# Second MLP product run one Strassen product after the other, with PSUM sums over the whole contraction and eight units begun early

## Chip, cores and metric

The kernel runs on one core of a Trainium2 chip. The metric is the device time of one launch in microseconds (us); lower is better.

## What is computed

A trunk of two layers over 1040 tokens (16 meta tokens and 1024 of the sequence): an SSD mixer and an MLP, then latent attention (MLA) and a second MLP. All is float32. The change touches the two MLPs only.

```python
D_MODEL = 1024; D_FF = 4 * D_MODEL
def sqrelu_mlp(h, w_up, w_down):
    return jnp.square(jax.nn.relu(h @ w_up)) @ w_down
# per layer:  h = h + mixer(rms_norm(h, ln_mix));  h = h + sqrelu_mlp(rms_norm(h, ln_mlp), w_up, w_down)
# out = h[:, N_META:]
```

## The kernel before

**Strassen.** `mlp(layer, ...)` (L557) forms each of its two products with the Winograd form of Strassen's scheme: both operands are cut in 2 x 2 blocks, and seven products P1 to P7 of blocks and of sums of blocks are made in place of eight. The token axis is cut in two halves of n columns (520 in layer 0, as two pieces of 260; 512 in layer 1). Each float32 product is three fp32r matmuls (L602 to L604: hi x hi, hi x lo, lo x hi), so every operand is split into a rounded part hi (ScalarE casts: L594 for weights, L743 for activations) and a rest lo (a subtraction: L596 for weights, in turn on GpSimd and VectorE; L744 for activations, on GpSimd).

**Up part.** 16 units of 256 hidden rows; each runs its seven products over 4 chunks of 128, that is 24 matmuls of 260 columns a product in layer 0 and 12 of 512 columns in layer 1. The weight loads (`raw`, L637), all hidden stores (L673, L688 to L695, into `hid`) and every other DMA of the MLP are issued by SyncE's queue, in order. Before the units can run, the head of the MLP has to make the sums of the activation blocks for P4 to P7 (`x_sums`, L797 to L817, with four lo parts on GpSimd a call, L744) while TensorE runs P1 and P2 of the first NPRE = 4 units, whose operands are plain blocks; GpSimd also sums the squares for the norm there (L754). P1's result waits in SBUF (`pu`, NPRE + 1 buffers) till the unit is finished later.

**Down part.** The contraction over 4096 hidden rows is cut in five parts of 4, 4, 3, 3 and 2 unit rows (DCH). In each part all seven products run (DORDER), each into PSUM tiles of its own (`mps`; four in layer 0, eight in layer 1), and each result is moved into the SBUF sums M: a copy in the first part (L1007), an addition on VectorE in the others (L1009), the joining sums of the last part on VectorE and GpSimd (L1014, L1032). The residual is added by VectorE from a DMA copy in layer 0 (L979, L980), and in layer 1 by matmuls with an identity ahead of the first part's products P2 to P5 (L997), whose tiles `ht` are loaded by DMA and partly changed on VectorE (L993, L995). Sums of weight blocks s1 and s2 are made on VectorE (L928 to L934) and kept in SBUF. The hidden block of a product is loaded (L901), cast as one instruction of 4n columns a lane (L903), and its lo part taken as one instruction too (L904), on GpSimd for five products of seven.

The order of each engine's queue comes from a scheduler that sorts the program by what is ready; `ahead` (L965) prepares weights four items ahead, loads twelve.

## Time and profile before

| | us |
|---|---|
| median of 3 runs | 3090.19 (3084.61 to 3090.22) |
| profiled execution | 3085.05 |
| its span | 3083.3 |
| TensorE busy in the span | 2924.2 (95%) |
| VectorE / GpSimd / ScalarE busy | 2365.5 / 1479.9 / 1298.1 |

MLP of layer 0: head from 976, units to about 1325, down part to 1695. MLP of layer 1: head from 2385, units to about 2715, down part to 3083. In the rows a chunk of time is given from the start of the span; "PEclk" is the granted TensorE clock as a share of full speed (2.4 GHz); a busy TensorE isn't a TensorE at its full rate, so a stretch is read by its number of matmuls too.

### The profile page before, as it was taken

The page shows a single profiled execution, that of the slowest core. Times are in us where ns is not written, and L with a number is a line of the kernel's source. Part 1 is how long each engine was busy: PE and PEld are TensorE (multiplying, and loading weights), DVE is VectorE, ACT ScalarE, POOL GpSimd, SP SyncE. Part 2 cuts the span into 40 slices and gives each one's busy share as a digit, 9 for nine tenths or more (in the row PEclk, how much of TensorE's full clock was granted, in tenths as well). Part 3 has the DMA queues.
Part 4 walks back from the last instruction along what each step waited for, and adds up shares of the span by engine and source line. Part 5 has one row for each costly group of instructions (what it writes and reads, how often), then busy time and mean ns, then how long its engine had stood idle before and what let it go on. Part 6 is the DMA issues. An engine that isn't in the chain of part 4 may idle for free.

```text
span 3083.3 us, 48544 instructions
## 1 busy us (share of the span) xinstructions
PE 2924.2 (95%) x18221; PEld 2604.8 (84%) x18221; DVE 2365.5 (77%) x3843; ACT 1298.1 (42%) x2453; POOL 1479.9 (48%) x1168
## 2 busy tenths in 40 slices
PE   7999999999999899999998889999999899989998
PEld 7999999998899799999998777777777688867886
DVE  6677887778667877777879477877865899865778
ACT  4343433334424433344332546655543533344342
POOL 2344544446746422245556454553655622243556
PEclk9999999999999899999999989999999899999999
DMA  3333433335533344464532201101223354464342
GB/s 107 70 75 68 77 66 74 74 74 130 153 97 118 117 160 142 149 234 143 169 119 85 60 22 26 26 25 27 92 80 100 99 191 161 154 231 158 121 146 96
DMA packets 290997, 332.72 MB, mean 108 GB/s; under 512 B 29981, under 2 KB 189682, under 8 KB 290762
## 3 DMA queue, kind: packets, MB, share of 16 engines
q1 hardware_dynamic: 290762, 329.62, 36.1%
q8 instruction: 144, 2.36, 0.3%
q14 instruction: 91, 0.75, 0.1%
HBM read 240.43 MB, written 89.07 MB: 107 GB/s over the span
## 4 chain that ended last, share of the span: by engine, by line
PE 69%; DVE 19%; DMA 4%; issue 4%; ACT 2%; POOL 2%; SPq 0%; DVEq 0%; ACTq 0%; POOLq 0%
PE mps L602 8%; PE mps L604 8%; PE mps L603 8%; PE psm L98 6%; PE psm L100 6%; PE psm L99 6%; PE mps L1058 2%; PE mps L1059 2%; PE mps L1060 2%; DVE em L378 2%; DVE whl L596 1%; PE ppv L1440 1%; PE pst L1426 1%; DVE xT L244 1%; DVE mP L1009 1%
## 5 line engine op out<-in xcount | busy, mean ns | idle before, releaser
L602 PE MATMUL mps<-hhl,whl 128*128 128x260 f32 (+1 forms) x1472 | 447.7, 304 | 25.0 <-DVE mP L1009 19.0
L603 PE MATMUL mps<-hhl,whl 128*128 128x260 f32 (+1 forms) x1472 | 443.8, 302 | 1.5 <-POOL hhl L744 1.5
L604 PE MATMUL mps<-hhl,whl 128*128 128x260 f32 (+1 forms) x1472 | 441.6, 301 | 2.4 <-DVE whl L596 2.1
L98 PE MATMUL psm<-hn,whl 128*128 128x346 f32 (+4 forms) x1176 | 387.4, 330 | 1.9 <-ACT hn L220 1.2
L99 PE MATMUL psm<-hn,whl 128*128 128x346 f32 (+4 forms) x1176 | 384.9, 328 | 0.3 <-DVE hn L221 0.3
L100 PE MATMUL psm<-hn,whl 128*128 128x346 f32 (+4 forms) x1176 | 380.9, 325 | 1.1 <-POOL whl L93 1.1
L602 PEld LDWEIGHTS mps<-hhl,whl 128*128 128x128 f32 x1472 | 283.9, 193 | 37.5 <-issue 17.7
L604 PEld LDWEIGHTS mps<-hhl,whl 128*128 128x128 f32 x1472 | 284.7, 194 | 11.1 <-DVE whl L596 3.2
L603 PEld LDWEIGHTS mps<-hhl,whl 128*128 128x128 f32 x1472 | 283.9, 193 | 11.0 <-POOL hhl L744 3.0
L93 POOL TENSOR_TENSOR whl<-wraw,whl 128x1024 fp32r<-128x1024 f32 (+3 forms) x95 | 221.6, 2334 | 142.3 <-ACT whl L90 135.9
L602 PE MATMUL mps<-xP,whl 128*128 128x260 f32 (+1 forms) x768 | 252.7, 329 | 17.5 <-ACT xP L743 7.6
L603 PE MATMUL mps<-xP,whl 128*128 128x260 f32 (+1 forms) x768 | 251.9, 328 | 2.1 <-POOL xP L744 2.1
L604 PE MATMUL mps<-xP,whl 128*128 128x260 f32 (+1 forms) x768 | 250.5, 326 | 0.9 <-DVE whl L596 0.9
L596 POOL TENSOR_TENSOR whl<-s,whl 128x512 fp32r<-128x512 f32 (+2 forms) x84 | 119.5, 1422 | 252.3 <-ACT whl L594 162.9
L98 PEld LDWEIGHTS psm<-hn,whl 128*128 128x128 f32 (+1 forms) x1176 | 219.4, 187 | 9.8 <-ACT btk L397 3.5
L904 POOL TENSOR_TENSOR hhl<-raw,hhl 128x2080 fp32r<-128x2080 f32 (+5 forms) x50 | 199.3, 3986 | 55.7 <-ACT hhl L903 49.6
L100 PEld LDWEIGHTS psm<-hn,whl 128*128 128x128 f32 (+1 forms) x1176 | 219.3, 187 | 6.2 <-issue 3.3
L99 PEld LDWEIGHTS psm<-hn,whl 128*128 128x128 f32 (+1 forms) x1176 | 219.8, 187 | 4.8 <-issue 1.7
L596 POOL TENSOR_TENSOR whl<-draw,whl 128x512 fp32r<-128x512 f32 (+2 forms) x90 | 123.8, 1379 | 184.7 <-ACT whl L594 142.2
L596 POOL TENSOR_TENSOR whl<-raw,whl 128x512 fp32r<-128x512 f32 x64 | 96.3, 1507 | 239.0 <-ACT whl L594 128.9
L594 ACT CAST whl<-draw 128x512 fp32r<-128x512 f32 (+2 forms) x180 | 102.4, 574 | 214.0 <-PE mps L1060 107.4
L1058 PE MATMUL mps<-whl,hhl 128*128 128x512 f32 x448 | 177.9, 402 | 15.2 <-DVE mP L1009 9.6
(388 smaller groups left out, 8498.0 us busy)
## 6 DMA issues: line engine op xcount, KB each, us to landing
raw<-in_mlp_w_up_dram SPq DMA_DIRECT2D x32, 1024.0 KB
hid<-stg SPq DMA_DIRECT2D x96, 260.0 KB
wraw<-in_ssd_w_in_dram SPq DMA_DIRECT2D x48, 512.0 KB
hid<-stg SPq DMA_DIRECT2D x96, 256.0 KB
acsb<-acs_d SPq DMA_DIRECT2D x64, 256.0 KB
draw<-in_mlp_w_down_dram SPq DMA_DIRECT2D x16, 1024.0 KB
raw<-hid SPq DMA_DIRECT2D x14, 1040.0 KB
raw<-hid SPq DMA_DIRECT2D x14, 1024.0 KB
```

The lines of the kernel that those rows point to most:

```text
L93: eng_lo.tensor_tensor(lo, src, hi.bitcast(F32), ALU.subtract)
L98: PE.matmul(ps, whi, xhi, start=i == 0, stop=False)
L99: PE.matmul(ps, whi, xlo, start=False, stop=False)
L100: PE.matmul(ps, wlo, xhi, start=False, stop=i == n - 1)
L378: V.tensor_tensor(em[:n, :, :n], em[:n, :, :n], cbm[:n, :n].unsqueeze(1).to_broadcast([n, HPG, n]), ALU.mult)
L594: S.copy(wt[:, 0], src)
L596: (G if lo_n[0] % 2 else V).tensor_tensor(wt[:, 1], src, wt[:, 0].bitcast(F32), ALU.subtract)
L602: PE.matmul(ps[:, i, :], wt[:, 0, k, :], xt[:, k, 0, xs_], start=first, stop=False)
L603: PE.matmul(ps[:, i, :], wt[:, 0, k, :], xt[:, k, 1, xs_], start=False, stop=False)
L604: PE.matmul(ps[:, i, :], wt[:, 1, k, :], xt[:, k, 0, xs_], start=False, stop=last)
L904: (G if p not in ("P5", "P6") else V).tensor_tensor(xt[:, :, 1, :], raw, xt[:, :, 0, :].bitcast(F32), ALU.subtract)
L1058: PE.matmul(ps[:, 0, :], xt[:, k, 0, qs], wt[:, 0, 0, :], start=k == 0 and not res, stop=False)
```

## The change

Parts of the diff; the old down part (L865 to L1083) is shown above and goes entirely.

```diff
-    DCH = (4, 4, 3, 3, 2)
-    NPRE = 4
+    NC = 4
+    HOME = {"P2": (0, 0), "P3": (0, 1), "P4": (1, 0), "P5": (1, 1)}
+    NPRE = 8
...
+        p1_d = dram.tile([NPRE, P, n], F32, name=f"p1_{layer}")
...
-        def w_item(src):
+        def w_item(src, on_v=False):
...
-            (G if lo_n[0] % 2 else V).tensor_tensor(wt[:, 1], src, wt[:, 0].bitcast(F32), ALU.subtract)
+            (G if lo_n[0] % 2 and not on_v else V).tensor_tensor(wt[:, 1], src, wt[:, 0].bitcast(F32), ALU.subtract)
...
             def prep(self, p):
+                if p == "P6" and self.u < NPRE:
+                    self.p1 = pu()
+                    nc.sync.dma_start(self.p1, p1_d[self.u])
...
                     S.copy(v3(self.p1), ps)
+                    if self.u < NPRE:
+                        nc.sync.dma_start(p1_d[self.u], self.p1)
...
-            if i % 2:
-                x_sums(i // 2)
+            if i % 4 == 3:
+                x_sums(i // 4)
...
+        if by_tok:
+            PHASES = [([A11], {"P1": (0, [])}),
+                      ([A21, A22, A11], {"P6": (2, [(0, 0, 1, ADD, None), (2, 0, 2, SUB, "s2")]), "P5": (0, [])}),
+                      ([A11, A21, A22], {"P7": (0, [(0, 0, 1, SUB, None)]), "P4": (2, [])}),
+                      ([A12, "s2"], {"P2": (0, []), "P3": (1, [(1, 0, 1, SUB, None)])})]
+        else:
+            PHASES = [([A11], {"P1": (0, [])}), ([A11, A21], {"P7": (0, [(0, 0, 1, SUB, "s3")])}),
+                      ([A12], {"P2": (0, [])}), ([A22, "s3"], {"P6": (0, [(0, 0, 1, SUB, "s2")])}),
+                      ([A22], {"P4": (0, [])}), ([A21, A22], {"P5": (0, [(0, 0, 1, ADD, None)])}),
+                      ([A12, "s2"], {"P3": (0, [(0, 0, 1, SUB, None)])})]
...
+        drb = dn.enter_context(tc.tile_pool(reuse_waits="tile", name="drawb", bufs=2))
...
+        drp = [dn.enter_context(tc.tile_pool(reuse_waits="tile", name=f"draw{i}", bufs=1)) for i in range(5)]
...
+                if isinstance(what, str):
+                    nc.sync.dma_start(t, s_d[what][c])
+                else:
+                    rows = w_down[layer, c * 1024:(c + 1) * 1024, what[0] * 512:(what[0] + 1) * 512]
+                    nc.sync.dma_start(t, rows.rearrange("(k j p) m -> j p k m", p=P, j=2)[what[1]])
...
+            for k in range(4):
+                S.copy(xt[:, k, 0, :], raw[:, k, :])
+                V.tensor_tensor(xt[:, k, 1, :], raw[:, k, :], xt[:, k, 0, :].bitcast(F32), ALU.subtract)
...
+            for o, a_, b_, op, keep in sums:
+                V.tensor_tensor(r[o], r[a_], r[b_], op)
+                if keep and i == 3:
+                    nc.sync.dma_start(s_d[keep][c], R[f, c][o])
+            return w_item(r[mine], True)
...
+            while dpos[0] < min(groups.index((f, c)) + (2 if by_tok else 3), len(groups)):
+                dload(*groups[dpos[0]])
...
+            while dpos[1] < min(j + 2, len(prods)):
+                hload(*prods[dpos[1]])
...
+            if j == 1 and not by_tok:
+                for p_, (i, half) in HOME.items():
+                    nc.sync.dma_start(M[p_], hsp[:, 4 * i:4 * i + 4, half, :])
+            if by_tok and c == 1 and p in HOME:
+                for q in range(4):
+                    residual(p, q, ps[q])
```

Eight units instead of four have P1 and P2 run in the head. P1's result goes to DRAM (`p1_d`) and comes back when the unit is finished. The four calls of `x_sums` are spread over sixteen products instead of eight.

The down part now runs in phases (a phase holds one product, or two in layer 1); in each, the contraction is taken in NC = 4 chunks of four unit rows into the same four PSUM tiles, and the tile is moved out once, in the last chunk (`evict`). A weight block is loaded again in every phase that uses it: 44 loads of 1024 KB in layer 0 and 36 in layer 1, where before each of the four blocks was loaded once, in five pieces. s2 (both layers) and s3 = A11 - A21 (layer 0) are stored to DRAM, four stores each, and loaded again; these loads are among the 44 and 36. All lo parts of the down part are taken on VectorE, those of the hidden blocks as four instructions. In layer 0 the residual is loaded into M ahead of the sums; in layer 1 its matmuls stand in the second chunk.

In these rows `raw` is a block loaded by DMA, `whl` and `hhl` are split weights and activations, `xP` the split activations of P4, P5 and P7 (P6's are in `hhl`), `t`, `ta` and `tb` activation sums, `rb` the sum of squares.

GpSimd in the head of layer 0's MLP, from the second call of `x_sums` on. Before:

```order
L754 TENSOR_TENSOR rb<-rb,sq 128x520
L596 TENSOR_TENSOR whl<-s_10722,whl 128x512
L754 TENSOR_TENSOR rb<-rb,sq 128x520
L744 TENSOR_TENSOR xP_10318<-t_10541,xP_10318 128x520
L754 TENSOR_TENSOR rb<-rb,sq 128x520
L744 TENSOR_TENSOR hhl<-t_10542,hhl 128x520
L596 TENSOR_TENSOR whl<-s_10720,whl 128x512
L754 TENSOR_TENSOR rb<-rb,sq 128x520
L744 TENSOR_TENSOR xP_10319<-tb,xP_10319 128x520
L744 TENSOR_TENSOR xP_10317<-ta,xP_10317 128x520
L596 TENSOR_TENSOR whl<-s_10722,whl 128x512
L744 TENSOR_TENSOR xP_10318<-t_10618,xP_10318 128x520
```

Now:

```order
L767 TENSOR_TENSOR rb<-rb,sq 128x520
L598 TENSOR_TENSOR whl<-raw,whl 128x512
L767 TENSOR_TENSOR rb<-rb,sq 128x520
L757 TENSOR_TENSOR xP_10321<-t_10680,xP_10321 128x520
L767 TENSOR_TENSOR rb<-rb,sq 128x520
L757 TENSOR_TENSOR hhl<-t_10681,hhl 128x520
L598 TENSOR_TENSOR whl<-raw,whl 128x512
L767 TENSOR_TENSOR rb<-rb,sq 128x520
L757 TENSOR_TENSOR xP_10317<-ta,xP_10317 128x520
L757 TENSOR_TENSOR xP_10325<-tb,xP_10325 128x520
L598 TENSOR_TENSOR whl<-raw,whl 128x512
L757 TENSOR_TENSOR xP_10321<-t_10831,xP_10321 128x520
```

The sixteen L744 (now L757) and seven L754 (now L767) are the same; four lo parts of P1 weights of units 4 to 7 (L598 from `raw`) now stand between the sums, where the lo parts of unit 0's sums `s` stood, which come later.

VectorE inside the down part of layer 0; before in the second part (P4, P2's residual, P5, P3), where `mP` are the sums M and `mps` PSUM tiles:

```order
L596 TENSOR_TENSOR whl<-draw,whl 128x512
L1009 TENSOR_TENSOR mP_14376<-mP_14376,mps 128x520
L934 TENSOR_TENSOR draw<-draw,s_14383 128x4x128 x2
L1009 TENSOR_TENSOR mP_14376<-mP_14376,mps 128x520
L596 TENSOR_TENSOR whl<-draw,whl 128x512
L934 TENSOR_TENSOR draw<-draw,s_14383 128x4x128
L1009 TENSOR_TENSOR mP_14376<-mP_14376,mps 128x520
L1009 TENSOR_TENSOR mP_14372<-mP_14372,mps 128x520
L596 TENSOR_TENSOR whl<-s_14383,whl 128x512
L1009 TENSOR_TENSOR mP_14372<-mP_14372,mps 128x520
L980 TENSOR_TENSOR mP_14372<-mP_14372,raw 128x2080
L1009 TENSOR_TENSOR mP_14372<-mP_14372,mps 128x520
```

Now, in the phase of P2 and P6, L947 being the weight sums:

```order
L598 TENSOR_TENSOR whl<-draw,whl 128x512
L947 TENSOR_TENSOR draw<-draw,drawb 128x4x128 x4
L598 TENSOR_TENSOR whl<-draw,whl 128x512 x3
L939 TENSOR_TENSOR hhl<-raw,hhl 128x520 x4
L598 TENSOR_TENSOR whl<-draw,whl 128x512
L947 TENSOR_TENSOR draw<-draw,drawb 128x4x128 x4
L598 TENSOR_TENSOR whl<-draw,whl 128x512 x3
L939 TENSOR_TENSOR hhl<-raw,hhl 128x520 x3
L995 TENSOR_TENSOR mP_14418<-mP_14418,mps 128x520
L939 TENSOR_TENSOR hhl<-raw,hhl 128x520
L598 TENSOR_TENSOR whl<-draw,whl 128x512
L995 TENSOR_TENSOR mP_14418<-mP_14418,mps 128x520
```

An M addition (L1009) per PSUM tile stood between the lo parts; now lo parts of weights (L598) and of hidden blocks (L939) and the sums follow each other, and additions (L995) come with a product's last chunk only.

SyncE's queue where layer 0 goes from the units to the down part; before, with L895 the weight blocks, L901 the hidden blocks, and L673 to L695 the last units' stores:

```order
L895 DMA draw<-in_mlp_w_down_dram 128x4x512 x2
L673 DMA hid_4_10286<-stg 128x520
L895 DMA draw<-in_mlp_w_down_dram 128x4x512 x2
L901 DMA raw<-hid_0_10282 128x4x520
L895 DMA draw<-in_mlp_w_down_dram 128x4x512
L901 DMA raw<-hid_0_10282 128x4x520
L673 DMA hid_4_10286<-stg 128x520
L688 DMA hid_4_10286<-stg 128x520
L690 DMA hid_4_10286<-stg 128x520
L692 DMA hid_4_10286<-stg 128x520
L695 DMA hid_4_10286<-stg 128x520
L895 DMA draw<-in_mlp_w_down_dram 128x4x512
```

Now:

```order
L928 DMA drawb<-in_mlp_w_down_dram 128x4x512
L706 DMA hid_3_10285<-stg 128x520
L928 DMA draw<-in_mlp_w_down_dram 128x4x512
L933 DMA raw<-hid_1_10283 128x4x520
L928 DMA draw<-in_mlp_w_down_dram 128x4x512
L928 DMA drawb<-in_mlp_w_down_dram 128x4x512
L949 DMA s_0_14448<-draw 128x2048
L933 DMA raw<-hid_2_10284 128x4x520
L1052 DMA mP_14418<-hsp_10287 128x4x520
L1052 DMA mP_14419<-hsp_10287 128x4x520
L1052 DMA mP_14420<-hsp_10287 128x4x520
L1052 DMA mP_14421<-hsp_10287 128x4x520
```

Behind the last unit's stores stand the blocks of the P7 phase (L928, two a chunk), the s3 store (L949) and the four loads of M (L1052), with the next hidden blocks (L933) among them.

## Rows read from the trace of the kernel before

**Rows 1.** The page: busy time of TensorE, PEld its weight loads.

```profile
PE 2924.2 (95%) x18221; PEld 2604.8 (84%) x18221; DVE 2365.5 (77%) x3843; ACT 1298.1 (42%) x2453; POOL 1479.9 (48%) x1168
```

**Rows 2.** Windows: length, each engine's busy time (instructions), PEclk, DMA share, GB/s.

```profile
976.00:1077.00 101.00, 86.40 (x580) 81.32 (x579) 90.24 (x104) 54.85 (x89) 59.46 (x36) 0.85 0.37 125
1077.00:1308.00 231.00, 231.00 (x1928) 231.00 (x1927) 180.20 (x263) 81.66 (x138) 59.92 (x40) 1.00 0.45 152
1308.00:1389.00 81.00, 74.67 (x580) 73.72 (x579) 58.93 (x55) 37.24 (x53) 37.81 (x16) 0.94 0.65 227
...
1500.00:1585.00 85.00, 78.21 (x615) 77.67 (x615) 69.15 (x77) 29.44 (x42) 43.71 (x24) 0.94 0.54 175
1585.00:1695.00 110.00, 98.11 (x772) 96.78 (x770) 95.45 (x132) 34.33 (x60) 67.88 (x46) 0.95 0.30 87
2385.00:2456.00 71.00, 60.00 (x198) 40.44 (x197) 64.05 (x66) 43.40 (x71) 51.47 (x32) 0.78 0.34 111
2456.00:2696.00 240.00, 240.00 (x1061) 198.72 (x1060) 213.62 (x304) 89.16 (x156) 63.05 (x44) 1.00 0.49 164
2696.00:2762.00 66.00, 53.27 (x225) 43.78 (x224) 43.70 (x49) 24.80 (x35) 29.16 (x11) 0.90 0.70 251
2762.00:2848.00 86.00, 79.51 (x385) 66.36 (x384) 44.33 (x40) 36.92 (x52) 36.45 (x17) 0.96 0.50 159
...
3044.00:3083.00 39.00, 25.53 (x97) 19.60 (x95) 35.97 (x41) 4.39 (x6) 22.82 (x13) 0.87 0.32 112
```

**Rows 3.** TensorE's waits, MLP of layer 0, then layer 1: total, times, longest.

```profile
PE mps L602 <- DVE mP L1009: 19.0, 10, 4.8
...
PE mps L1058 <- DVE mP L1009: 9.6, 3, 7.6
PE mps L997 <- DMA ht<-hsp: 7.1, 2, 4.9
```

**Rows 4.** Windows, layer 0 head: L744, L754, L596 (DVE, POOL); all engines.

```profile
976.00:1038.00 62.00, 28.81 (x16) 0.79 0.31 103
...
976.00:1038.00 62.00, 11.73 (x7) 0.79 0.31 103
...
976.00:1038.00 62.00, 9.60 (x8) 12.78 (x8) 0.79 0.31 103
...
1004.00:1039.00 35.00, 25.93 (x102) 22.07 (x103) 28.05 (x27) 17.80 (x30) 28.03 (x18) 0.61 0.18 63
```

**Rows 5.** Timeline: start, duration; VectorE, then GpSimd, layer 0 down part.

```profile
1351.71 0.68 DVE L929 TENSOR_TENSOR s<-s,draw 128x512 f32<-128x512 f32 x1
...
1354.02 5.19 DVE L929 TENSOR_TENSOR s<-s,draw 128x512 f32<-128x512 f32 x1
...
1353.94 4.72 POOL L904 TENSOR_TENSOR hhl<-raw,hhl 128x2080 fp32r<-128x2080 f32 x1 [0.40 <-POOL whl L596]
```

**Rows 6.** Layer 0 down part, VectorE, then GpSimd: busy, mean ns, idle before.

```profile
L1009 DVE TENSOR_TENSOR mP<-mP,mps 128x520 f32<-128x520 f32 x110 | 74.3, 687 | 26.6 <-PE mps L604 26.0
L596 DVE TENSOR_TENSOR whl<-draw,whl 128x512 fp32r<-128x512 f32 x20 | 30.0, 1506 | 17.5 <-ACT whl L594 17.5
...
L904 POOL TENSOR_TENSOR hhl<-raw,hhl 128x2080 fp32r<-128x2080 f32 x10 | 47.9, 4786 | 11.1 <-ACT hhl L903 10.6 <-POOL whl L596 0.4
```

**Rows 7.** Windows of 12 us at DMA peaks, columns as in rows 2.

```profile
1332.00:1344.00 12.00, 8.35 (x41) 7.81 (x42) 10.32 (x11) 3.75 (x7) 4.65 (x3) 0.72 1.05 405
1500.00:1512.00 12.00, 11.50 (x96) 11.32 (x96) 9.29 (x9) 2.69 (x4) 4.39 (x4) 1.00 1.01 360
1512.00:1524.00 12.00, 8.49 (x50) 8.31 (x50) 11.69 (x11) 4.99 (x7) 8.19 (x4) 0.72 0.60 189
```

**Rows 8.** Window of a unit stretch in layer 1, as rows 2.

```profile
2478.00:2500.00 22.00, 22.00 (x99) 18.22 (x98) 21.87 (x34) 7.98 (x15) 4.25 (x3) 1.00 0.58 196
```

**Rows 9.** Timeline near the end: VectorE's joining sums; TensorE's last matmul.

```profile
3058.98 10.83 DVE L1014 TENSOR_TENSOR mP<-mP,mP 128x512 f32<-128x512 f32 x8
...
3078.71 0.39 PE L1060 MATMUL mps<-whl,hhl 128*128 128x512 f32 x1
```

More of the change, by code (lines that the diff above doesn't have):

```diff
@@ L565, in mlp @@
         hslice = [slice(t0, t0 + n) for t0 in tok]
-        hid_d = [dram.tile([u_n, 7, P, n], F32, name=f"hid{layer}_{c}") for c, u_n in enumerate(DCH)]
+        hid_d = [dram.tile([4, 7, P, n], F32, name=f"hid{layer}_{c}") for c in range(NC)]
+        p1_d = dram.tile([NPRE, P, n], F32, name=f"p1_{layer}")
         hsp = dram.tile([P, KD, 2, n], F32, name=f"hsp{layer}")
@@ L631, in __init__ @@
                 self.S, self.W, self.C, self.A = {}, {}, {}, None
-                self.c = next(c for c in range(len(DCH)) if u < sum(DCH[:c + 1]))
-                self.d = hid_d[self.c][u - sum(DCH[:self.c])]
+                self.d = hid_d[u // 4][u % 4]
             def load(self):
@@ new lines, in mlp, with draw, dload @@
+        turn = [0]
+        def draw():
+            turn[0] += 1
+            return drp[(turn[0] - 1) % 5].tile([P, 4, 512], F32, name="draw")
+        s_d = {s_: dram.tile([NC, P, 4, 512], F32, name=f"{s_}_{layer}") for s_ in ("s2", "s3")}
+        groups = [(f, c) for f in range(len(PHASES)) for c in range(NC)]
+        prods = [(f, c, p) for f, c in groups for p in PHASES[f][1]]
+        R = {}
+        XH = {}
+        def dload(f, c):
+            R[f, c] = []
+            for j, what in enumerate(PHASES[f][0]):
+                t = drb.tile([P, 4, 512], F32, name="drawb") if j == 1 else draw()
+                if isinstance(what, str):
[3 more added lines that the diff above has]
+                    nc.sync.dma_start(t, rows.rearrange("(k j p) m -> j p k m", p=P, j=2)[what[1]])
+                R[f, c].append(t)
@@ L1040, in mlp, with evict, add, more @@
-        i = 0
-        for c, p in prods:
-            nk = parts[c].nk
-            res = by_tok and c == 0 and p in HOME
+                PE.matmul(ps[:, 0, j * P:(j + 1) * P], t[:, j, :], ident, start=False, stop=False)
+        def evict(p, q, ps):
+            m = {j: M[f"P{j}"][:, q, :] for j in range(1, 8) if f"P{j}" in M}
+            def add(out_, a, op=ALU.add):
+                V.tensor_tensor(v3(out_), v3(a), ps, op)
+            def more(out_, a):
+                G.tensor_tensor(out_, out_, a, ALU.add)
+            def store(t, p_):
+                i, half = HOME[p_]
+                nc.sync.dma_start(out[0, half * 512 + q * P:half * 512 + (q + 1) * P, i * 512:(i + 1) * 512], t)
+            def stored(p_, a, op=ALU.add):
+                t = outp.tile([P, n], F32, name="mo")
+                add(t, a, op)
+                store(t, p_)
+            if p == "P1":
+                S.copy(v3(m[1]), ps)
+                if not by_tok:
+                    more(m[2], m[1])
+            elif by_tok:
+                if p == "P6":
+                    add(m[6], m[1])
+                elif p == "P5":
+                    S.copy(v3(m[5]), ps)
+                elif p == "P7":
+                    add(m[7], m[6])
+                    more(m[6], m[5])
+                    more(m[5], m[7])
+                    store(m[5], "P5")
+                elif p == "P4":
+                    stored("P4", m[7], ALU.subtract)
+                elif p == "P2":
+                    stored("P2", m[1])
+                else:
+                    stored("P3", m[6])
+            elif p == "P7":
+                S.copy(v3(m[7]), ps)
+            elif p == "P6":
+                add(m[1], m[1])
+                more(m[7], m[1])
+                more(m[4], m[7])
+                more(m[5], m[7])
+            elif p == "P5":
+                add(m[1], m[1])
+                more(m[3], m[1])
+                add(m[5], m[5])
+            else:
+                j = int(p[1])
+                add(m[j], m[j], ALU.subtract if p == "P4" else ALU.add)
@@ new lines, in mlp @@
+        pss = {}
+        for j, g in enumerate(prods):
+            f, c, p = g
+            if c == 0:
+                pss[p] = [psum() for _ in range(4)]
+            ps, end = pss[p], c == NC - 1
+            if j == 1 and not by_tok:
[4 more added lines that the diff above has]
+                    residual(p, q, ps[q])
@@ L1079, in mlp @@
-            for q in range(4):
-                close(c, p, q, pss[q])
+                    ahead(j, q)
+                    for k in range(4):
+                        mm_k(ps[q], wts[g, q], XH[p, c], k, c == 0 and k == 0, end and k == 3)
+                    if end:
+                        evict(p, q, ps[q])
+            elif not end:
+                for k in range(4):
+                    ahead(j, k)
+                    for q in range(4):
+                        mm_t(ps[q], wts[g, k], XH[p, c], k, q, c == 0 and k == 0, False)
+            else:
+                ahead(j, 3)
+                for q in range(4):
+                    for k in range(4):
+                        mm_t(ps[q], wts[g, k], XH[p, c], k, q, False, k == 3)
+                    evict(p, q, ps[q])
```

209 lines of the change are left out of this document (42 added, 167 removed).

## Prediction, made blind

> **What bounds the kernel now.** I began with the page: TensorE is busy 95% of the span [rows 1], so time can only be won where it isn't at its full rate. Busy time doesn't show that, since a matmul at half clock counts as busy; so I next cut both MLPs into windows and compared the number of matmuls with the length [rows 2]. Two windows are steady, with a granted clock of 1.00 (2.4 GHz): 1928 matmuls of 260 columns in 231.0 us, 0.1198 us each, and 1061 of 512 columns in 240.0 us, 0.2262 us each. Length minus number times that spacing is what a window loses, to waits and to the lower clock behind them:
>
> Layer 0: head (976 to 1077) 101 - 580 x 0.1198 = 31.5; start of the down part (1308 to 1389) 11.5; its middle (1500 to 1585) 11.3; its end (1585 to 1695) 17.5. The down part loses 40.3.
>
> Layer 1: head (2385 to 2456) 71 - 198 x 0.2262 = 26.2; 2696 to 2848 holds 610 matmuls, of which 128 are the residual's of 128 columns, which I estimate at half the spacing: 152 - 482 x 0.2262 - 128 x 0.113 = 28.5; the end (3044 to 3083) 39 - 97 x 0.2262 = 17.1, of which 4.6 lies behind the last matmul at 3078.7 [rows 9] and stays: 12.5. The down part loses 41.0.
>
> In all 57.7 us in the heads and 81.3 in the down parts: 139 us. This is the most that the change can give, 3085 - 139 = 2946, since the matmuls stay the same. The waits name who is late [rows 3]: above all VectorE's additions into M (L1009), 19.0 us in layer 0 and 9.6 in layer 1, and in layer 1 the residual's DMA with 7.1.
>
> **The heads.** Between 1004 and 1039 GpSimd is busy for 28.0 of 35 us while the granted clock is 0.61 and TensorE does 102 matmuls, worth 12.2 us [rows 4]. GpSimd's work till the sums are ready is 16 lo parts (28.8 us), 7 additions of squares (11.7) and lo parts of weights (12.8), 53 of 62 us [rows 4]. The change doesn't shorten this chain; the order shows four lo parts of units 4 to 7 where three of unit 0's stood, so the sums come at about the same time, at most 4 x 12.8 / 8 = 6.4 us later. What it gives is work to wait with: eight more products of 24 matmuls, 8 x 24 x 0.1198 = 23.0 us in layer 0 and 8 x 12 x 0.2262 = 21.7 in layer 1, taken from later, where TensorE runs at full rate. Of the 31.5 and 26.2 us lost, these can cover 23 and 21.7 at most. They need lo parts from the same GpSimd queue, behind the sums: I put some 4 us of stalls there. That gives 19 in layer 0; in layer 1, where less is lost, 16. Bounds: 5 each, if the new lo parts come as late as the sums do, and 25 and 22 if everything fits.
>
> The price later is hidden: the eight units then lack two products each to cover the same VectorE work. VectorE is full for 21.9 of 22 us in such a stretch of layer 1, and TensorE still does 99 matmuls, 0.222 us each [rows 8]; so four more such units cost nothing till VectorE's backlog outgrows the three products of lead. I take 0 and keep 8 us for the range. The P1 results' way through DRAM (8 stores and 8 loads of 260 KB a layer) lies beside work at a DMA share of 0.45 [rows 2].
>
> **The down parts, VectorE.** Taken out: 224 L1009, of which the 110 timed in layer 0 cost 687 ns each [rows 6], against some 44 evictions now, so a PSUM tile is no longer waited for in every product. Added: all lo parts on VectorE. What makes them affordable is a stall that the trace shows: a 0.68 us sum took 5.19 us while GpSimd ran a 4.72 us lo part of a hidden block [rows 5]. The lo parts of weights (L596) took 1506 ns on average, against 680 ns for the undisturbed sum of the same shape [rows 5, 6]. The long lo parts on GpSimd go away. A product of layer 0 (96 matmuls, 11.5 us) now asks VectorE for 4 lo parts of weights, 4 of hidden blocks and up to 4 sums, 12 x 0.68 = 8.2 us, in its last chunk 4 evictions more, 10.9. In layer 1 (48 matmuls, 10.9 us) P6 asks for 16 x 0.68 = 10.9, but P5 runs in turn with it and asks for 5.4. VectorE keeps up, by a third on average. If GpSimd's joins (28 in layer 0, short of 2 us each) block it, one product at a phase's end is late: 3 us a layer.
>
> **The down parts, DMA.** This is where I was least sure. The cover of the reloads is free bandwidth, 0.43 to 0.70 of which is used now in most windows [rows 2]. A product of P7 in layer 0 needs two weight blocks, a hidden block and a store of s3: 4.2 MB in 11.5 us, 365 GB/s. P1 and P7 together, with the four loads of M, need 28 such transfers, 29.4 MB in 92 us, 320 GB/s. The trace shows 405 GB/s at a share of 1.05, so it fits, with 10% to spare in P7; loads run three groups ahead. But a burst of 360 GB/s at 1500 was followed by a window with 50 matmuls in 12 us, 6 us lost [rows 7]. Something like this will remain at each start of a down part, where the last units' stores, the first blocks and the hidden blocks meet in SyncE's queue: I leave 4 us there in layer 0 and 5 in layer 1, 3 inside each, and 1 at the very end, where VectorE's eight joining sums (10.8 us, [rows 9]) no longer stand ahead of the last product. Left: 7 of 40.3 and 9 of 41.0, so 33 + 32 are gained. Bounds: 31 in all if five or six more stalls of the 6 us kind come in, and 77.
>
> The residual costs nothing in layer 0 (the loads replace L980) and its 128 matmuls stay in layer 1, but their tiles now have a product's time to arrive.
>
> **Sum.** 19 + 16 + 33 + 32 = 100 us; 3085 - 100 = **2985 us**, made against the profiled execution, which lies 5 us under the median of the three runs shown; a median of the changed kernel may be as much above.
>
> **Rivals.**
> (a) DMA becomes the wait. In the P7 and P6 phases of layer 0 blocks arrive late, some 5 to 6 stalls of 6 us (wait and low clock together, [rows 7]): 2985 + 33 = 3018. For it: 365 GB/s asked, and the windows behind the bursts. Against: 405 seen, and the lead.
> The Trainium skill, page "DMA: Bandwidth & Descriptors", section "Bandwidth", puts the limit between HBM and SBUF at about 358 GB/s for a core when the memory's other core streams too, and 435 at the fabric. By the first figure the P7 phase would be DMA bound; the trace's 405 GB/s lies above it, so here the measurement decides, and the rule leaves this rival at its chance.
> (b) The heads stay bound by GpSimd, and the new products only wait in their turn: 5 us each in place of 19 and 16, so 2985 + 25 = 3010. For it: GpSimd is full there, and its work grows by four lo parts.
> (c) Slower. SyncE issues in order; a hidden block's load stands behind a weight load that waits until its buffer (`drawb`, two of them) is read by the sums, and the next product's lo parts wait for that block. If that happens in regular rhythm, each time costs the 6 us of [rows 7]; there are 56 products, and from 100 / 6 = 17 stalls, about one product in three, the gain is gone. At one in two it is 28 x 6 - 100 = 68 us slower, 3153. For it: the order puts M's four loads and s3's stores between hidden blocks. Against: `draw` has five buffers, and the loads are placed two products early.
> (d) No change: the lost time comes back elsewhere, as low clock behind new waits, 3085. Nothing in the rows points to it.
>
> **Chances and range.** The forecast 0.62, (a) 0.16, (b) 0.12, (c) 0.07, (d) 0.03. (a) and (b) together would be 3043. The range goes from near the ceiling, 2948, to 3045. A change within 0.2% (6 us), about what a measurement of this kernel can tell from none, is (d). Faster 0.90, same 0.03, slower 0.07.
>
> **What would show it.** In the changed profile: the head of layer 0 with a granted clock near 0.95 rather than 0.85; no wait for additions into M; lo parts of weights near 0.7 us; the down parts at 0.12 and 0.226 us a matmul, with DMA at 250 to 370 GB/s. I am wrong if TensorE's waits name DMA for `raw` or `drawb` in product after product, or if the low clock stays in the heads.

## The result, and the profile after

The changed kernel takes **3005.0 us** in the median of four runs (3000.68 to 3009.95), against 3089.66 (3084.61 to 3090.22, four runs): a ratio of 0.973, 95% interval 0.9709 to 0.9751. It is 85 us faster; forecast were 100 (2985, range 2948 to 3045).

The page of after, busy times as in [rows 1]. The number of matmuls is the same, TensorE is busy for 42 us less in a span that is 77 shorter, and GpSimd has lost a quarter of its work:

```profile
PE 2882.3 (96%) x18221; PEld 2579.1 (86%) x18221; DVE 2231.1 (74%) x3904; ACT 1283.4 (43%) x2539; POOL 1114.1 (37%) x996
```

Windows of both MLPs, columns as in [rows 2]: in layer 0 head, units, down part; then the same in layer 1.

```profile
982.40:1094.30 111.90, 97.98 (x777) 96.09 (x778) 100.56 (x112) 61.59 (x102) 63.36 (x40) 0.97 0.51 169
1094.30:1326.10 231.80, 230.63 (x1922) 230.44 (x1921) 194.89 (x284) 84.81 (x146) 55.46 (x38) 1.00 0.53 182
1326.10:1655.40 329.30, 324.59 (x2689) 323.47 (x2688) 212.43 (x327) 128.87 (x227) 34.56 (x24) 0.99 0.75 274
2352.00:2456.90 104.90, 95.28 (x390) 75.38 (x389) 94.99 (x107) 61.78 (x103) 63.11 (x40) 0.93 0.50 166
2456.90:2679.40 222.50, 219.38 (x961) 179.60 (x960) 199.76 (x291) 82.22 (x146) 54.94 (x38) 1.00 0.56 192
2679.40:3002.30 322.90, 320.40 (x1473) 266.05 (x1472) 196.66 (x312) 125.73 (x221) 11.77 (x8) 1.00 0.67 239
```

I read them as before: length minus number of matmuls by 0.1198 or 0.2262 us. Layer 0 loses 111.9 - 777 x 0.1198 = 18.8 in the head, 1.5 in the units, 329.3 - 2689 x 0.1198 = 7.2 in the down part. Layer 1 loses 16.7, 5.1 and, with the 128 matmuls of the residual at half the spacing, 322.9 - 1345 x 0.2262 - 14.5 = 4.2. In all 53.5 us, where it was 139: 85.5 us are gained. The down parts run at a granted clock of 0.99 and 1.00, where the windows of [rows 2] stood at 0.87 to 0.96.

TensorE's waits, layer 0 and then layer 1, total, times, longest; to be held against [rows 3]:

```profile
PE mps L604 <- DVE pu L710: 4.3, 3, 2.6
PE mps L604 <- DVE c L710: 4.2, 2, 2.2
PE mps L606 <- DVE whl L598: 3.4, 1, 3.4
PE mps L604 <- ACT xP L756: 3.4, 1, 3.4
...
PE mps L604 <- ACT hhl L938: 1.2, 1, 1.2
...
PE mps L606 <- DVE whl L598: 6.3, 6, 3.2
PE mps L606 <- POOL whl L598: 3.8, 2, 2.3
...
PE mps L611 <- ACT whl L596: 2.1, 3, 0.7
```

The additions into M are gone from the list, and so is the residual's DMA. What is left stands in the heads and units, but for the 3.4 us for `whl` (L606) and the 1.2 us for `hhl` (L938) in the down part of layer 0 and the 2.1 us of L611 in that of layer 1.

The profiled execution took 3008.28 us and is one of the two slower of the four. It holds a wait in the SSD part, at about 102 us, that the profile of before hardly has; after first, then before:

```profile
PE psm L98 <- DVE zs L269: 4.4, 1, 4.4
```

```profile
PE psm L98 <- DVE zs L269: 0.4, 1, 0.4
```

The change doesn't touch that part, and the MLP of layer 0 starts at 982 instead of 977. The attention between the MLPs took 690 us in the profile of before and 697 in that of after; in the eleven kernels below, whose attention is the same, it took 683 to 697. Neither difference is laid to the change; runs of one kernel spread over 10 us and more, so medians are compared below, and losses are read inside the MLPs.

### The profile page after: what moved, and what is told of

Its sections match the earlier page's. It is cut to its first block, busy times and chain, and to the rows that moved or that the text cites. A ratio compares the mean times of both kernels' runs of the same rounds, so it can differ in the third digit from the quotient of the medians.

```text
span 3006.6 us, 48412 instructions
## 1 busy us (share of the span) xinstructions
PE 2882.3 (96%) x18221; PEld 2579.1 (86%) x18221; DVE 2231.1 (74%) x3904; ACT 1283.4 (43%) x2539; POOL 1114.1 (37%) x996
## 5 line engine op out<-in xcount | busy, mean ns | idle before, releaser
L604 PE MATMUL mps<-hhl,whl 128*128 128x260 f32 (+1 forms) x1472 | 440.5, 300 | 8.5 <-DVE c L710 4.2
L606 PE MATMUL mps<-hhl,whl 128*128 128x260 f32 (+1 forms) x1472 | 436.6, 297 | 8.0 <-DVE whl L598 4.3
L605 PE MATMUL mps<-hhl,whl 128*128 128x260 f32 (+1 forms) x1472 | 437.7, 298 | 0.1
L604 PEld LDWEIGHTS mps<-hhl,whl 128*128 128x128 f32 x1472 | 278.0, 189 | 19.1 <-issue 4.8
L606 PEld LDWEIGHTS mps<-hhl,whl 128*128 128x128 f32 x1472 | 279.0, 190 | 17.8 <-DVE whl L598 5.4
L605 PEld LDWEIGHTS mps<-hhl,whl 128*128 128x128 f32 x1472 | 278.2, 189 | 8.5 <-issue 0.5
L598 DVE TENSOR_TENSOR whl<-draw,whl 128x512 fp32r<-128x512 f32 x208 | 150.4, 735 | 172.5 <-ACT whl L596 172.4
L596 ACT CAST whl<-draw 128x512 fp32r<-128x512 f32 x208 | 128.7, 622 | 324.8 <-PE mps L606 169.8
L604 PE MATMUL mps<-xP,whl 128*128 128x260 f32 (+1 forms) x768 | 246.5, 321 | 11.1 <-ACT xP L756 3.4
L606 PE MATMUL mps<-xP,whl 128*128 128x260 f32 (+1 forms) x768 | 245.9, 321 | 5.4 <-DVE whl L598 5.4
L605 PE MATMUL mps<-xP,whl 128*128 128x260 f32 (+1 forms) x768 | 246.1, 320 | 0.0
L998 POOL TENSOR_TENSOR mP<-mP,mP 128x520 f32<-128x520 f32 (+1 forms) x28 | 43.3, 1568 | 492.5 <-DVE mP L995 432.6
L598 POOL TENSOR_TENSOR whl<-raw,whl 128x512 fp32r<-128x512 f32 x64 | 95.4, 1494 | 217.8 <-ACT whl L596 96.5
L612 PE MATMUL mps<-whl,hhl 128*128 128x512 f32 x448 | 173.8, 389 | 0.3 <-DVE whl L598 0.3
L613 PE MATMUL mps<-whl,hhl 128*128 128x512 f32 x448 | 174.0, 389 | 0.0
```

The source lines that it names most:

```text
L596: S.copy(wt[:, 0], src)
L598: (G if lo_n[0] % 2 and not on_v else V).tensor_tensor(wt[:, 1], src, wt[:, 0].bitcast(F32), ALU.subtract)
L604: PE.matmul(ps[:, i, :], wt[:, 0, k, :], xt[:, k, 0, xs_], start=first, stop=False)
L605: PE.matmul(ps[:, i, :], wt[:, 0, k, :], xt[:, k, 1, xs_], start=False, stop=False)
L606: PE.matmul(ps[:, i, :], wt[:, 1, k, :], xt[:, k, 0, xs_], start=False, stop=last)
L612: PE.matmul(ps[:, 0, :], xt[:, k, 0, qs], wt[:, 1, 0, :], start=False, stop=False)
```

## Experiments

The table gives the loss against steady issue for stretches of equal work: the first 768 matmuls of layer 0's MLP (head), the next 1920 (units) and the last 2688 (down), and 384, 960 and 1344 in layer 1, each time length minus number by spacing (and minus 14.5 us for the residual's matmuls in layer 1). The wait where units turn into the down part counts as units here. Medians are of four runs (seven for e_head_only), before had 3089.25, 3086.42 and 3089.18 us beside the three sets.

| kernel | median us | ratio to before, interval | layer 0: head, units, down | layer 1: head, units, down |
|---|---|---|---|---|
| before | 3089.66 | | 32.0, 4.7, 37.3 | 27.7, 6.3, 37.6 |
| after | 3005.0 | 0.973 (0.9709 to 0.9751) | 19.9, 1.8, 7.4 | 18.0, 5.4, 4.6 |
| e_down_only | 3022.57 | 0.9781 (0.9747 to 0.9814) | 30.5, 0.2, 7.2 | 28.1, 0.8, 8.0 |
| e_head_only | 3073.56 | 0.9942 (0.9923 to 0.9961) | 20.6, 6.6, 34.4 | 18.3, 11.2, 39.9 |
| e_lo_as_before | 3044.59 | 0.9851 (0.9826 to 0.9877) | 20.1, 4.0, 25.6 | 17.8, 8.1, 19.1 |
| e_old_lo_v | 3061.58 | 0.9915 (0.9889 to 0.9941) | 34.3, 4.6, 21.3 | 26.6, 5.4, 28.6 |
| e_hid_twice | 3047.07 | 0.9871 (0.9849 to 0.9893) | 20.1, 5.4, 32.0 | 18.0, 9.8, 18.7 |
| e_npre6 | 3014.93 | 0.9767 (0.9744 to 0.979) | 24.3, 0.5, 8.3 | 24.1, 2.3, 9.4 |
| e_up_lo_v | 2987.53 | 0.9684 (0.9657 to 0.9711) | 19.7, 0.4, 6.1 | 15.0, 0.4, 4.7 |
| e_all_lo_v | 2974.98 | 0.9631 (0.959 to 0.9672) | 9.6, 0.4, 6.9 | 4.5, 0.4, 4.5 |
| e_lo_v_npre4 | 2995.19 | 0.9697 (0.9673 to 0.9722) | 22.2, 0.2, 6.7 | 18.7, 0.4, 4.8 |
| e_joins_v | 2963.08 | 0.9588 (0.9564 to 0.9612) | 10.1, 0.4, -0.4 | 5.5, 0.9, 4.9 |
| e_old_all_lo_v | 3042.82 | 0.9857 (0.9834 to 0.988) | 20.7, 4.8, 21.2 | 19.0, 4.3, 26.8 |

### The two halves, each alone

The new down part with the old head, as edits of the changed kernel:

```diff
-    NPRE = 8
+    NPRE = 4
...
-                if p == "P6" and self.u < NPRE:
-                    self.p1 = pu()
-                    nc.sync.dma_start(self.p1, p1_d[self.u])
...
-                    if self.u < NPRE:
-                        nc.sync.dma_start(p1_d[self.u], self.p1)
...
-            if i % 4 == 3:
-                x_sums(i // 4)
+            if i % 2:
+                x_sums(i // 2)
```

> The new down part with the old head: four units begun early, sums every second product, P1 results kept in SBUF. Theory: the two halves of the change are independent, and in the changed trace the down parts account for 34 us in layer 0 and 39 us in layer 1 of what TensorE lost before, so 3085 - 73 = 3012 us; the loss in the heads is back at 32 and 28 us, and no loss in the stretch of units of layer 1. Rival: the head's gain is what the units and the latent attention give back, so without it the time is no worse than with it, 3000 to 3005 us.

And the other way round: all lines of the change that concern the up part (units, P1's way through DRAM, the head's loads and pools) set into the kernel before, with these two edits among them:

```diff
-    NPRE = 4
+    NPRE = 8
...
-            if i % 2:
-                x_sums(i // 2)
+            if i % 4 == 3:
+                x_sums(i // 4)
```

> The old down part with the new head: eight units begun early, sums every fourth product, P1 results through DRAM. Theory: 12 us gained in the head of layer 0, 10 in that of layer 1, less 5 us lost later in the units of layer 1 where VectorE is full: 3085 - 17 = 3068 us. By the blind estimate of the heads alone (19 + 16 us, nothing given back) it would be 3050 us. Rival: the units of layer 1 give everything back, 3080 us.

Measured: 3022.6 and 3073.6 us, 67 and 16 below before; together 82, and the whole change gives 85. The halves are independent, and the rival of the first run falls: without the new head the time is 18 us worse. Both theories count from 3085, the profiled execution; against the median of before beside them, 3089.25, the gains are 67 us where 73 were expected and 16 where 17 were, and the blind estimate of the heads would have given 35. In the table one sees where: the heads lose 20.6 and 18.3, not 13 and 10, and the units of layer 1, with the turn to the down part, 11.2 where it was 6.3.

### Where the lo parts run

The changed kernel with the old places of the lo parts in its down part:

```diff
-            for k in range(4):
-                S.copy(xt[:, k, 0, :], raw[:, k, :])
-                V.tensor_tensor(xt[:, k, 1, :], raw[:, k, :], xt[:, k, 0, :].bitcast(F32), ALU.subtract)
+            S.copy(xt[:, :, 0, :], raw)
+            (G if p not in ("P5", "P6") else V).tensor_tensor(xt[:, :, 1, :], raw, xt[:, :, 0, :].bitcast(F32), ALU.subtract)
...
-            return w_item(r[mine], True)
+            return w_item(r[mine])
```

> The changed kernel, but in the down parts the lo parts are where they were: weights in turn on GpSimd and VectorE, hidden blocks in one instruction, on GpSimd for five products of seven. Theory: GpSimd and VectorE hold each other up, so lo parts of weights on VectorE are back at 1.2 to 1.5 us and lo parts of hidden blocks at 4.8 us, but with few evictions left TensorE waits only where a product's first weights are late: some 20 us over both layers, 3020 to 3030 us. Rival: the evictions were the whole cause, and where the lo parts run doesn't matter, 3000 to 3008 us.

And the kernel before with the new places in its old down part (the other calls of `w_item` there get `True` too):

```diff
-                S.copy(xt[:, :, 0, :], raw)
-                (G if p not in ("P5", "P6") else V).tensor_tensor(xt[:, :, 1, :], raw, xt[:, :, 0, :].bitcast(F32),
-                                                                 ALU.subtract)
+                for k in range(self.nk):
+                    S.copy(xt[:, k, 0, :], raw[:, k, :])
+                    V.tensor_tensor(xt[:, k, 1, :], raw[:, k, :], xt[:, k, 0, :].bitcast(F32), ALU.subtract)
...
-                    return w_item(a(*AT[p]))
+                    return w_item(a(*AT[p]), True)
...
```

> The kernel before, with one thing changed: in the down parts all lo parts run on VectorE, those of hidden blocks in one instruction per 128 rows. Theory: VectorE then has 224 additions into M, 56 joining sums and all lo parts; without the hold-ups from GpSimd it comes out about full in the down parts, so the time stays within 20 us of before, 3065 to 3105 us. Rival: the hold-ups between GpSimd and VectorE were the whole cause, the evictions none, and it falls to 3030 us or less.

Measured: 3044.6, which is 40 us above the changed kernel, and 3061.6, which is 28 below before. The theory of the first had the direction and half the size, 20 us; that of the second missed, since it kept the time within 20 us of before, and its rival, 3030 us or less, is further off still. The two edits of the down part can so be priced in both orders. Moving the lo parts is worth 28 us on the old loops and 40 on the new; the phases are worth 29 us with the old lo parts (3073.6 to 3044.6) and 39 with the new (3061.6 to 3022.6). Neither is the whole cause; each makes the other worth some 10 us more. Two things are not separated. With the engine, both runs also change the hidden blocks' cast and lo part between four instructions and one; in e_lo_as_before TensorE waits 5.5 us in layer 0 for `hhl` of L938, the long instruction, so part of the 28 and 40 us may be due to the cut in four. And the phases bring fewer evictions, another place for the residual and another order of loads at once.

VectorE's groups in the down part of layer 0, busy time, mean ns, idle before; after, then e_lo_as_before with GpSimd's longest group (L946 is L947 there, L938 is L939):

```profile
L598 DVE TENSOR_TENSOR whl<-draw,whl 128x512 fp32r<-128x512 f32 x112 | 83.1, 749 | 95.0 <-ACT whl L596 95.0
L939 DVE TENSOR_TENSOR hhl<-raw,hhl 128x520 fp32r<-128x520 f32 x101 | 71.8, 766 | 0.0
L947 DVE TENSOR_TENSOR draw<-draw,drawb 128x512 f32<-128x512 f32 x64 | 43.9, 745 | 6.4 <-issue 3.0 <-DMA draw<-in_mlp_w_down_dram 2.9 <-DVE whl L598 0.4
```

```profile
L598 DVE TENSOR_TENSOR whl<-draw,whl 128x512 fp32r<-128x512 f32 x56 | 80.4, 1439 | 104.0 <-ACT whl L596 97.2 <-DMA raw<-hid 4.6 <-DMA drawb<-in_mlp_w_down_dram 2.2
L946 DVE TENSOR_TENSOR draw<-draw,drawb 128x512 f32<-128x512 f32 x64 | 79.1, 1293 | 22.3 <-DMA draw<-in_mlp_w_down_dram 16.1 <-issue 6.3
...
L938 POOL TENSOR_TENSOR hhl<-raw,hhl 128x2080 fp32r<-128x2080 f32 x18 | 86.7, 4817 | 23.0 <-ACT hhl L937 23.0
```

The same subtraction takes 749 ns on average where GpSimd is nearly idle and 1439 where it shares the work; the weight sums, which nobody moved or cut, go from 745 to 1293: that part is GpSimd's doing. With the lo parts divided, VectorE's two groups need 160 us for 120 instructions; alone it does all 277 of the three groups in 199.

### The room left on the DMA

```diff
             nc.sync.dma_start(XH[p, c], hid_d[c][:, ORDER.index(p)].rearrange("u p n -> p u n"))
+            nc.sync.dma_start(XH[p, c], hid_d[c][:, ORDER.index(p)].rearrange("u p n -> p u n"))
```

> The changed kernel with every hidden block of the down parts loaded twice into the same tile: 28 loads of 1.04 MB more in each layer, nothing else. Theory: the DMA has some 10% to spare in the phases of P1 and P7 in layer 0 (29.4 MB in 92 us against 405 GB/s seen); with 8 loads more these two want 37.9 MB, 412 GB/s, so blocks come late there and TensorE loses 15 to 20 us, in layer 1 5 to 10: 3025 to 3035 us. Rival: the DMA has room, and at most 5 us are lost, up to 3010 us. Third: the loads are at the limit already, and each us of DMA added shows, 8.5 MB at 405 GB/s = 21 us in the first two phases and 50 us in all, 3055 us.

Measured: 3047.1, 42 us more than the changed kernel, between theory and third case. The first 100 us of the down part of layer 0 in the changed kernel, with 50 us of it, columns as in [rows 2]:

```profile
1325.00:1425.00 100.00, 99.97 (x833) 99.54 (x832) 57.64 (x89) 41.23 (x74) 6.01 (x4) 1.00 0.99 383
...
1350.00:1400.00 50.00, 50.00 (x421) 50.00 (x420) 31.14 (x46) 19.31 (x34) 6.01 (x4) 1.00 1.04 410
```

And the same stretch of e_hid_twice, a late one of its down part, and TensorE's longest wait (start, duration, then in brackets the wait):

```profile
1325.00:1425.00 100.00, 81.47 (x624) 80.44 (x623) 47.78 (x73) 32.03 (x58) 5.21 (x4) 0.88 1.01 389
1600.00:1678.00 78.00, 78.00 (x654) 78.00 (x653) 50.23 (x90) 29.18 (x53) 8.66 (x8) 1.00 0.69 236
...
1388.04 1.24 PE L604 MATMUL mps<-hhl,whl 128*128 128x260 f32 x4 [13.99 <-ACT hhl L939]
```

The second load (L934) of a tile stands in SyncE's queue until the first has landed; total, times, longest, in 1320 to 1430 and then in 1600 to 1678:

```profile
SPq L934 <- DMA raw<-hid: 23.2, 4, 7.3
...
SPq L934 <- DMA raw<-hid: 30.8, 4, 9.0
```

The changed kernel's DMA was already full: share 0.99 for 100 us, 1.04 and 410 GB/s for 50 us, while TensorE did 421 matmuls, 0.119 us each. It lost nothing there: the waits name no late block, so the loads ran far enough ahead. With the hidden blocks twice the rate hardly grows, 389 GB/s, the lead is used up, and one block is 14 us late. Late in the down part, at 236 GB/s, the second load costs nothing (78.0 us for 654 matmuls) though SyncE's queue waits even longer there, so it is the rate, and not the time of a single load or the queue's wait, that hurts.
The Trainium skill, page "DMA: Bandwidth & Descriptors", section "Bandwidth", gives some 358 GB/s for a core when its neighbour streams too and 425 measured with one alone; the 410 GB/s here agree with the second figure, and rule out the first as the limit of this case.

### How many units early

```diff
-    NPRE = 8
+    NPRE = 6
...
-            if i % 4 == 3:
-                x_sums(i // 4)
+            if i % 3 == 2:
+                x_sums(i // 3)
```

> The changed kernel with six units begun early in place of eight, the sums on every third product. Theory: the heads' loss lies between that with four (30 and 28 us) and eight (20 and 18), at 25 and 23, and the units of layer 1 lose 2 to 3 us instead of 5: 3005 + 7 = 3012 us. Rival: the last two units give nothing in the head, because its stalls come from queues on VectorE, and only cost in the units: 3000 us.

Measured: 3014.9, between four (3022.6) and eight (3005.0); the theory holds. Head of layer 0: 30.5, 24.3 and 19.9 us lost with four, six and eight; units of layer 1: 0.8, 2.3 and 5.4. The last two units still give 10 us in both heads together and cost some 4 in the units; the down part of layer 1 loses 4.8 us more with six than with eight, which neither side expected and no run explains.

### GpSimd out of the heads and units

```diff
-        def w_item(src, on_v=False):
+        def w_item(src, on_v=True):
```

> The changed kernel with the lo parts of the weights in the heads and units on VectorE too, none on GpSimd (the activation sums' lo parts stay there). Theory: a lo part on GpSimd costs VectorE more in hold-up (about 1 us) than it costs VectorE to make it (0.68 us), so VectorE gains time: the 5.0 us lost in the units of layer 1 go to 0 to 2, the heads (20 and 18 us) lose 3 less each: 2993 us. Rival: VectorE is the bound in heads and units and takes on more work: 10 us more in each head and the units lose time, 3025 us.

Then, on top of it, the lo parts of the activation sums:

```diff
-            G.tensor_tensor(xt[:, k, 1, :], src, xt[:, k, 0, :].bitcast(F32), ALU.subtract)
+            V.tensor_tensor(xt[:, k, 1, :], src, xt[:, k, 0, :].bitcast(F32), ALU.subtract)
```

> As the run before it, and also the lo parts of the activation sums in the heads on VectorE; GpSimd keeps the additions of squares alone. Theory of hold-ups: about 50 instructions on VectorE in the head take up to 1.8 us each beside GpSimd and 0.7 alone, so with the 30 moved ones it has 80 x 0.7 = 56 us, no more than its 56.5 now, and the sums are ready earlier: the heads lose 10 us each in place of 20 and 18, 2985 us. Rival: the two engines do share work, and one alone is late: heads lose 30 us each, 3027 us.

Measured: 2987.5 and 2975.0, 17 and 30 us below the changed kernel. In the first the units of both layers lose nothing any more (6.4 us) and the head of layer 1 loses 3.0 less, as its theory had it, that of layer 0 no less; the losses come to 11 us of the 17 in the medians. In the second the heads lose 9.6 and 4.5, where its theory had 10 each; that is 20.6 us less than in the first, where the medians differ by 12.6 (its own runs lie between 2960.6 and 2982.9). The first 63 us of layer 0's head in the changed kernel, e_up_lo_v and e_all_lo_v, columns as in [rows 2]:

```profile
982.00:1045.00 63.00, 51.83 (x409) 50.59 (x410) 56.49 (x51) 42.68 (x74) 52.65 (x33) 0.97 0.52 169
```

```profile
976.90:1039.90 63.00, 56.05 (x416) 54.59 (x417) 62.10 (x66) 44.66 (x77) 37.83 (x23) 0.91 0.51 169
```

```profile
982.00:1045.00 63.00, 62.04 (x506) 60.79 (x504) 62.31 (x91) 46.42 (x80) 11.06 (x7) 1.00 0.60 193
```

In e_up_lo_v GpSimd has 37.8 us of work in place of 52.7, and yet TensorE does no more than 416 matmuls in place of 409, with VectorE busy 62.1 of 63 us at 0.94 us an instruction: a shorter queue on GpSimd, paid for with more work on VectorE, gives nothing in this head. In e_all_lo_v VectorE does 91 instructions in 62.3 us where it did 51 in 56.5, 0.68 us each against 1.11; TensorE does 506 matmuls in the 63 us and not 409. Taking work from GpSimd and giving it to the engine that was full has made that engine faster.

Is the early start then still of use? The same kernel with the old head:

```diff
-    NPRE = 8
+    NPRE = 4
...
-            if i % 4 == 3:
-                x_sums(i // 4)
+            if i % 2:
+                x_sums(i // 2)
```

> All lo parts of the MLPs on VectorE, and again four units begun early (sums every second product, P1 results in SBUF): the run e_all_lo_v with the old head. Asks what the eight units are worth once GpSimd holds nothing up. Theory of hold-ups: the sums' chain is some 40 us of 0.7 us instructions on VectorE, and TensorE has 23 + 11.5 us of work meanwhile, so the head loses 6 to 10 us more than with eight units (9.6 and 4.4 us lost): 2982 to 2992 us. Rival: the chain is as long as on GpSimd and the early units are worth 12 and 10 us as before: 2997 us or more.

Measured: 2995.2, 20 us worse; the theory said 7 to 17, and its rival, 22 or more, is as near. The heads lose 22.2 and 18.7, that is 12.6 and 14.2 more, where the theory had 6 to 10 each and the rival 12 and 10: on the sizes the rival is the nearer one, and the early units are worth no less than before. Of the rival's reason only half holds. The chain on VectorE is shorter than on both engines (22.2 against 30.5 with four units), but it still is longer than the work of four units.

### The joins

On top of e_all_lo_v:

```diff
             def more(out_, a):
-                G.tensor_tensor(out_, out_, a, ALU.add)
+                V.tensor_tensor(out_, out_, a, ALU.add)
```

> As e_all_lo_v, and the joining sums of the down parts (28 in layer 0, 8 in layer 1) on VectorE instead of GpSimd. In layer 0, at the end of P6, twelve of these on GpSimd stretch four weight sums on VectorE to 6.3 us, and TensorE then waits 3.7 us and loses 7 us with the low clock. Theory: without them these 7 us go, 2968 us. Rival: 12 joins more of 0.68 us make that product's VectorE work 17 us against 11.5, and the stall stays or grows: 2975 to 2985 us.

The kernel has 20 of these joins in layer 0 and 8 in layer 1 (`more` in `evict`), not the 28 and 8 of the expectation, nor the 28 in layer 0 of the prediction; twelve at the end of P6 is right.

Measured: 2963.1, 12 us below e_all_lo_v, of which the trace shows 7.3 in the down part of layer 0 (6.9 to -0.4), as the theory had it. Over all six stretches it shows 4.9; the rest of the 12 us lies within the spread of e_all_lo_v's runs. The stall in question, in the changed kernel: VectorE, GpSimd and then TensorE at the end of P6, start and duration.

```profile
1516.79 1.80 DVE L598 TENSOR_TENSOR whl<-draw,whl 128x512 fp32r<-128x512 f32 x1
1518.52 1.80 DVE L939 TENSOR_TENSOR hhl<-raw,hhl 128x520 fp32r<-128x520 f32 x1
1520.24 0.68 DVE L995 TENSOR_TENSOR mP<-mP,mps 128x520 f32<-128x520 f32 x1
1520.85 6.30 DVE L947 TENSOR_TENSOR draw<-draw,drawb 128x512 f32<-128x512 f32 x4
...
1516.26 10.34 POOL L998 TENSOR_TENSOR mP<-mP,mP 128x520 f32<-128x520 f32 x6
...
1527.81 0.39 PE L606 MATMUL mps<-hhl,whl 128*128 128x260 f32 x1 [3.38 <-DVE whl L598]
```

The four weight sums (L947) take 6.30 us beside the joins, 2.5 in the run below; the next product's lo parts (L598) stand behind them and come late, which is the wait of 3.4 us in the list above; with the low clock behind it (0.77 granted from 1530 to 1535) 5.3 us are lost. In e_joins_v the sums take 2.49 us, with a lo part and four joins right behind them on the same engine:

```profile
1496.83 2.49 DVE L947 TENSOR_TENSOR draw<-draw,drawb 128x512 f32<-128x512 f32 x4
1499.23 0.68 DVE L598 TENSOR_TENSOR whl<-draw,whl 128x512 fp32r<-128x512 f32 x1
1499.84 2.52 DVE L998 TENSOR_TENSOR mP<-mP,mP 128x520 f32<-128x520 f32 x4
```

This kernel takes 0.9588 of before (0.9564 to 0.9612), clearly less than the changed kernel (0.973); the interval of e_all_lo_v (0.959 to 0.9672) overlaps it. GpSimd has only the additions of squares left in its MLPs.

### The engine's choice alone

The kernel before with all lo parts of both MLPs on VectorE, that is e_old_lo_v (its cut of the hidden blocks' lo parts in one instruction per 128 rows with it) and the two edits of the heads and units:

```diff
-        def w_item(src, on_v=False):
+        def w_item(src, on_v=True):
...
-            G.tensor_tensor(xt[:, k, 1, :], src, xt[:, k, 0, :].bitcast(F32), ALU.subtract)
+            V.tensor_tensor(xt[:, k, 1, :], src, xt[:, k, 0, :].bitcast(F32), ALU.subtract)
```

> The kernel before with all lo parts of both MLPs on VectorE, nothing else of the change: four units begun early, old down part with 224 additions into M. Asks how much of the whole the choice of the engine gives alone. Theory: in the down parts the 28 us measured for the kernel before with the down parts' lo parts moved, and in heads and units what the same moves gave on the changed kernel, 30 us, less some because only four units are begun early: 3035 to 3042 us. Rival: without the early units VectorE's chain is no shorter than GpSimd's, the heads lose 32 and 28 us as ever: 3055 to 3062 us.

Measured: 3042.8, just above the theory's 3035 to 3042; against the 3089.18 of before beside it that is a gain of 46 us, where the theory, counted from 3085, had 43 to 50. Half of what the whole change brought is to be had by naming another engine in a few lines.

## Why the prediction was right, point by point

**The method.** Loss against steady issue, 139 us, was the right account: the change took 85.5 of them. By the table's account of equal work, before lost 145.6 us, the changed kernel 57.1 (88.5 less), and e_joins_v, after the runs had moved the rest piece by piece, 21.4. What TensorE's busy time says (42 us less) would have missed half, since low clock counts as busy.

**The heads: right mechanism, too large a size.** Forecast 19 + 16, measured 31.5 - 18.8 = 12.7 and 26.2 - 16.7 = 9.5. I had put 4 us of stalls in layer 0 for lo parts that wait behind the sums on GpSimd. GpSimd's work in the head, L757, L767 and L598 (VectorE, then GpSimd), against [rows 4], and a stretch of it:

```profile
982.00:1045.00 63.00, 26.58 (x16) 0.97 0.52 169
...
982.00:1045.00 63.00, 12.25 (x7) 0.97 0.52 169
...
982.00:1045.00 63.00, 11.73 (x10) 14.55 (x10) 0.97 0.52 169
...
1009.00:1036.00 27.00, 22.32 (x180) 21.52 (x178) 23.82 (x24) 16.01 (x29) 21.03 (x13) 1.00 0.45 150
```

GpSimd's part came as said: the same sixteen and seven, lo parts of weights 14.6 us up to 1045, and the sums ready after 62 us instead of 56, within the 6.4 us that I allowed. What I left out is that GpSimd's instructions hold VectorE up, and that the eight early products bring VectorE more evictions and lo parts in the very stretch in which it is held up: 23.8 of 27 us busy, with 24 instructions, and TensorE at 180 matmuls of 225. The largest single piece lies behind that stretch. From 1034 to 1046 TensorE waits 3.4 us for a sum (`xP` of L756, in the list above) and 2.9 for an eviction on ScalarE (L714), both behind VectorE (L824 and L681), and does 34 matmuls in the 12 us, at a granted clock of 0.78: some 8 of the 18.8 us. I had priced the heads on GpSimd's queue alone; the row of the hold-up [rows 5] stood in my own argument for the down part and wasn't carried over. Against GpSimd's queue as the bound of layer 0's head speaks e_up_lo_v: the queue is over a quarter shorter there, the sums are ready after 55 us instead of 62, and the head loses the same. e_all_lo_v, which takes all lo parts from GpSimd, gains 10 and 13 us in the heads; how much of that is hold-up and how much the sums' own lo parts, done sooner, isn't separated.

**The units: priced at nothing, cost 5.** For layer 1 I took [rows 8] as proof that full units keep up, with 8 us kept for the range. They don't keep up for eight units in a row: 5.1 us, of which 3.1 are five waits of L606 for lo parts on VectorE (2457 to 2679; total, times, longest):

```profile
PE mps L606 <- DVE whl L598: 3.1, 5, 1.1
```

The runs with four, six and eight units show the dose (0.8, 2.3, 5.4). With eight units and no lo parts of weights on GpSimd it is 0.4 (e_up_lo_v), so the hold-up is what made VectorE fall behind. In layer 0 it was 1.5.

**The down parts: right in size, half wrong in the reasons.** Forecast 33 + 32, measured 40.3 - 7.2 = 33.1 in layer 0 and 41.0 - 4.2 = 36.8 in layer 1. That VectorE keeps up once GpSimd is out of its way was right, and the two runs from both sides (28 and 40 us) bear it out, though they hold the cut of the lo parts too. The stall at a phase's end by GpSimd's joins, 3 us a layer, came in layer 0 at the named place and cost 5.3. The residual lost its waits, as said. On the DMA I was right by luck: 320 GB/s with 10% to spare, I wrote; it was 383 GB/s for 100 us and nothing to spare, because the loads run ahead and bring the next phases' blocks into the same stretch (the loads of two s3 blocks for the P6 phase are issued at 1381 and 1395, while P7 runs). In the program they stand two groups and one product ahead (`+ 3` and `j + 2` count the one in use), not three and two as I wrote; the scheduler moves them further. The cover was the lead, not the spare rate. e_hid_twice shows how near rival (a) was: with 28 loads of 1.04 MB more a layer it comes true, at 42 us.

**The rivals.** (b), heads still bound, is the one that came halfway, though by VectorE and not by GpSimd's queue. (a) and (c) need late blocks, and TensorE's waits name none in the changed kernel. (d) has nothing behind it.

**The sum.** Heads 12.8 us less than forecast, units 6.6 less (1.5 in layer 0, 5.1 in layer 1), down parts 4.9 more: 100 - 14.5 = 85.5. The medians say 85.

## What to carry to other kernels

Price a helper engine by what it holds up, not by what it does: before giving a second engine half of a queue, look whether the same instruction on the first takes longer while the second runs, and if so, try giving it nothing. Count the loss of the bound engine against its own steady rate, stretch by stretch, since waits and the low clock after them don't show in busy time. And when a change spends bandwidth, add up what the prefetch brings into a stretch, not only what the stretch uses.
